# Alternating the two head groups in the chunk scan of a gated-DeltaNet layer

## The chip, the cores and the metric

The program runs on one NeuronCore of a Trainium2 chip, as a single launch. The metric is the device time of that launch in microseconds (us), lower is better. The engines are called as in the profile: PE is TensorE (its weight loads are shown apart as PEld), DVE is VectorE, ACT is ScalarE, POOL is GpSimd, and SP issues DMAs.

## The reference

A trunk of two layers over 512 tokens with 1024 features. Layer 0 is a gated-DeltaNet layer (6 heads of width 128), layer 1 is sliding-window attention; each is followed by a feed-forward part. The change concerns the DeltaNet layer alone. Its state update runs over chunks of tokens, one after the other for each head, and the heads do not depend on each other:

```python
def gated_delta_rule_chunked(q, k, v, g, beta):
    ...
    sol = lax.linalg.triangular_solve(lower, rhs, left_side=True, lower=True, unit_diagonal=True)
    u, w = sol[..., :dv], sol[..., dv:]
    ...
    def step(state, inp):
        u_n, w_n, a_n, qg_n, kg_n, gl_n = inp
        v_new = u_n - jnp.einsum("bhck,bhkv->bhcv", w_n, state)
        o_n = jnp.einsum("bhck,bhkv->bhcv", qg_n, state) + jnp.einsum("bhcs,bhsv->bhcv", a_n, v_new)
        state = state * gl_n[..., None, None] + jnp.einsum("bhck,bhcv->bhkv", kg_n, v_new)
        return state, o_n
```

Afterwards each head's output is normalised, multiplied by a gate `silu(z)`, and projected by `w_out` together with the memory attention.

## The kernel before, in words

Everything is held transposed: features on the 128 partitions, the 512 tokens along the free axis. A dense projection of one 128-wide output tile is 24 matmuls of 128x512: 8 pieces of the inner dimension, times three products, because weights and activations are split into a rounded high part (`whi`, `h`) and the rest (`wlo`, `l`). The function `mm3` issues the three; their results are the PSUM banks called `pj` or `g`. Each weight tile is loaded by SP (`wraw`), rounded by ACT (`whi`) and subtracted by DVE (`wlo`).

The kernel uses chunks of 128 tokens, so there are NC = 4 chunks for each of the 6 heads. The names in the rows of a trace are these: `kn` holds a head's keys, `kg` the decayed keys, `qg` the decayed queries (in the buffers `gcr`, where the output is written over them), `DT` the decayed query-key products, `Tt` the inverted triangles, `N` the values, `S` the state. One step of the scan, for one head and one chunk (`scan_step`, lines 771 to 797), is a chain of small matmuls and small operations of the other engines, all in one PSUM bank `sc`:

- PE `sc<-S,kn`, then DVE `R` (line 781); the first chunk has no state and starts at the next matmul with `N` in place of `R` (`sc<-N,Tt`);
- PE `sc<-R,Tt`, then ACT `vn` (a copy with a factor, line 784);
- PE `sc<-vn,kg`, then DVE `S`, the next state (lines 790, 792); the last chunk has none;
- PE `sc<-gcr,S` and `sc<-DT,vn` give the output, which ACT copies into `gcr` (line 796). Only then is the bank free.

There are three `sc` banks (`self.banks(pj=3, g=2, sc=3)`), and a step keeps one from its first matmul to its copy. A 128x128 matmul on f32 data is two records in the trace; a step has 3 (first chunk), 5, 5 and 4 (last chunk) matmuls, 17 for each head and 102 for the six.

The heads are handled in two groups, `first` (heads 0 to 2) and `second` (heads 3 to 5). `values(heads)` projects a group's values: for each head a projection `pj`, a convolution on ACT and DVE (`qv`), a Silu on ACT, four transposes on PE into a `g` bank and a multiplication on DVE into `N`. After the scan, `squares`, `total` and `finish` normalise a group's output: ACT squares it into `N`, DVE adds and multiplies with tiles that SP has loaded into the buffers of `kg` (`q2`) and `kn` (`z`), PE sums over the partitions with a matmul by `ones` (128x512 on f32 data), ACT takes Ln and Exp, DVE multiplies, and ACT and DVE split the result into `h` and `l`. `opened_rows` then multiplies the parts of the result that are ready by `w_out`, row by row.

The order of the instructions on each engine is not the order of the code. A scheduler of the language orders them when the program is built, by the code's order and by what each waits for; on the chip each engine takes its list strictly in that order. This is how matmuls of a projection come to stand between the steps of a scan. `self.use(LN_EXP)` (line 689) places a load of ACT's function table behind the last Silu and ahead of the first Ln.

Of the kernel before, what the change touches and what calls it, by code (L numbers as in the profile page):

```python
# [23 lines left out]
NC = 4  # L24
# [63 lines left out]
class Builder:  # L88
# [409 lines left out]
    def gdn(self, gp):  # L498
# [112 lines left out]
        for i in range(NH):  # L611
            h, c = divmod(i, NC)
# [14 lines left out]
        def values(heads):  # L627
            vs = {}

            def value(h):  # L630
                vs[h] = self.conv_tile(2 * H + h, self.t(gp, [P, T], F32, "qv", 5))
                self.fn(vs[h], vs[h], AF.Silu)

            value(heads[0])
            for h in heads:
                if h + 1 in heads:
                    value(h + 1)
                v = vs[h]
                ps = self.bank("g")
                for c in range(NC):  # L640
                    self.tr(ps[:, chunk(c)], v[:, chunk(c)])
                self.tt(nc.vector, N[h], c4(ps), wide(ir[h]), ALU.mult)
                vt.append(N[h])
# [4 lines left out]
        def scan(heads, chunks=range(NC)):  # L648
            for c in chunks:
                for h in heads:  # L650
                    S[h] = self.scan_step(gp, h, c, S[h], kn[h], Tt[h], kg[h], vt[h], qg[h], AT[h], br[h])
# [4 lines left out]
        def squares(heads):  # L656
            for h in heads:
                t, gate[h] = self.t(gp, [P, T], F32, f"kg{h}"), self.t(gp, [P, T], F32, f"kn{h}")
                nc.sync.dma_start(t, q2[h])
                nc.sync.dma_start(gate[h], z[h])  # L660
                sums[h], o = (x.rearrange("p c i -> p (c i)") for x in (N[h], qg[h]))
                self.square(sums[h], o)
                self.tt(nc.vector, sums[h], sums[h], t, ALU.add)
            for h in heads:
                o = qg[h].rearrange("p c i -> p (c i)")
                self.tt(nc.vector, o, o, gate[h], ALU.mult)
# [15 lines left out]
        first, second = range(0, 3), range(3, H)  # L682
        for heads in (first, second):
            self.solve(gp, heads, [N[h] for h in heads], X, [Tt[h] for h in heads])
        values(first)
        scan(first, range(NC - 1))
        values(second)
        scan(first, range(NC - 1, NC))
        self.use(LN_EXP)
        scan(second)  # L690
        squares(first)
        total(first, "g")
        finish(first)
# [688 lines left out]
```

## Time and profile before

| | |
|---|---|
| median of 3 runs | 1141.31 us (1141.19 to 1141.54) |
| the profiled execution | 1140.89 us |
| its span, from the first to the last instruction | 1139.0 us |
| PE busy | 1121.6 us, 98% of the span |
| DVE, ACT, POOL busy | 841.6, 632.1, 86.2 us |
| granted clock of TensorE, mean | 0.998 |

The profile's lists by time give the start of an instruction, its length, its engine, its line, what it writes and reads, and in brackets how long the engine stood idle before it and for whom. PE's lengths are modelled and overlap, so that its busy share stays near 100% where it waits for a tenth of a microsecond; its pace is read from one start to the next.

### The profile page before, as it was taken

The numbers are of one execution on the slowest core, as the hardware profiler recorded it, in microseconds if no ns is written. First come the engines' busy times: TensorE is split into PE (matmuls) and PEld (weight loads), VectorE is DVE, ScalarE is ACT, GpSimd is POOL, SyncE is SP. The second block draws the span as 40 slices with busy tenths as digits, with TensorE's granted clock in tenths as the row PEclk, the third lists the DMA queues.
The fourth block names the chain that finished last, engine by engine and source line by source line (L and its number), as shares of the span: only waits on it lengthen the run. The fifth ranks groups of instructions, "written<-read, shape, count | busy, mean of one in ns | idle before, by whom it ended". The sixth has DMA issues, their size and how long they took to land.

```text
span 1139.0 us, 19670 instructions
## 1 busy us (share of the span) xinstructions
PE 1121.6 (98%) x7476; PEld 992.7 (87%) x7476; DVE 841.6 (74%) x1592; ACT 632.1 (55%) x1274; POOL 86.2 (8%) x97
## 2 busy tenths in 40 slices
PE   7999999999999999999999999999999999999996
PEld 6888887887899998899998888888999988999986
DVE  6754887776889987389876868959799743899754
ACT  7569572365566653256653656855566522566533
POOL 0120000000101100011100000010011100111000
PEclk9999999999999999999999999999999999999999
DMA  8434342324667744567723421153477733677232
GB/s 311 128 114 113 120 107 98 95 91 148 188 145 188 186 129 126 159 146 188 185 72 93 134 74 57 43 133 122 126 183 179 199 98 106 150 185 185 70 99 91
DMA packets 73971, 152.76 MB, mean 134 GB/s; under 512 B 17756, under 2 KB 18420, under 8 KB 73876
## 3 DMA queue, kind: packets, MB, share of 16 engines
q1 hardware_dynamic: 62356, 130.52, 37.4%
q0 software_dynamic: 11520, 20.98, 11.7%
q8 instruction: 59, 0.97, 0.4%
q14 instruction: 36, 0.29, 0.1%
HBM read 144.51 MB, written 6.96 MB: 133 GB/s over the span
## 4 chain that ended last, share of the span: by engine, by line
PE 95%; DVE 2%; ACT 1%; DMA 1%; issue 0%; SPq 0%; DVEq 0%; ACTq 0%
PE pj L154 47%; PE g L154 37%; PE sc L154 6%; PE pt L154 2%; PE qk L154 2%; PE pt L168 1%; PE g L168 1%; DMA wraw<-in_wmk 1%; DVE wlo L171 1%; ACT whi L148 0%; ACT sm L142 0%; SPq L329 0%; DVE x L171 0%; DVE l L174 0%; DVE stats L836 0%
## 5 line engine op out<-in xcount | busy, mean ns | idle before, releaser
L148 ACT ACTIVATE whi<-wraw 128x512 fp32r<-128x512 f32 (+2 forms) x331 | 244.1, 746 | 241.9 <-PE pj L154 151.2
L171 DVE TENSOR_TENSOR wlo<-wraw,whi 128x512 fp32r<-128x512 f32 (+2 forms) x331 | 273.0, 835 | 105.8 <-ACT whi L148 99.8
L154 PE MATMUL pj<-h,whi 128*128 128x512 f32 (+1 forms) x676 | 265.4, 393 | 0.1
L154 PE MATMUL pj<-l,whi 128*128 128x512 f32 (+1 forms) x676 | 263.7, 390 | 0.0
L154 PE MATMUL pj<-h,wlo 128*128 128x512 f32 (+1 forms) x676 | 263.4, 390 | 0.0
L154 PE MATMUL g<-T,whi 128*128 128x256 f32 x1280 | 228.1, 278 | 0.2
L154 PEld LDWEIGHTS g<-T,whi 128*128 128x128 f32 x1280 | 194.7, 188 | 1.8 <-DVE fu L174 1.8
L154 PE MATMUL g<-T,wlo 128*128 128x256 f32 x640 | 177.8, 278 | 0.0
L154 PEld LDWEIGHTS pj<-h,whi 128*128 128x128 f32 x676 | 126.9, 188 | 28.4 <-issue 3.5
L154 PEld LDWEIGHTS pj<-h,wlo 128*128 128x128 f32 x676 | 127.0, 188 | 25.8 <-DVE wlo L171 0.4
L154 PEld LDWEIGHTS pj<-l,whi 128*128 128x128 f32 x676 | 127.1, 188 | 24.7 <-DVE l L171 0.4
L154 PE MATMUL g<-h,whi 128*128 128x256 f32 (+1 forms) x492 | 138.4, 281 | 0.0
L154 PE MATMUL g<-h,wlo 128*128 128x256 f32 (+1 forms) x492 | 138.0, 280 | 0.0
L154 PE MATMUL g<-l,whi 128*128 128x256 f32 (+1 forms) x492 | 138.0, 280 | 0.0
L154 PEld LDWEIGHTS g<-T,wlo 128*128 128x128 f32 x640 | 120.1, 188 | 0.0
L154 PEld LDWEIGHTS g<-l,whi 128*128 128x128 f32 x492 | 92.3, 188 | 0.8 <-issue 0.2
L154 PEld LDWEIGHTS g<-h,whi 128*128 128x128 f32 x492 | 92.3, 188 | 0.8 <-issue 0.2
L154 PEld LDWEIGHTS g<-h,wlo 128*128 128x128 f32 x492 | 92.3, 188 | 0.5
L1104 POOL DMA_DIRECT2D ws<-in_wgu x40 | 35.3, 882 | 705.7 <-ACT sq L151 237.7
L148 ACT ACTIVATE whi<-ws 128x512 fp32r<-128x512 f32 x80 | 50.4, 631 | 49.3 <-PE g L154 40.2
L171 DVE TENSOR_TENSOR fu<-pj,rstd 128x512 f32<-128x512 f32 (+1 forms) x34 | 22.4, 660 | 54.3 <-PE pj L154 54.2
L171 DVE TENSOR_TENSOR wlo<-ws,whi 128x512 fp32r<-128x512 f32 x80 | 54.9, 686 | 6.4 <-ACT whi L148 6.3
(384 smaller groups left out, 1649.4 us busy)
## 6 DMA issues: line engine op xcount, KB each, us to landing
wraw<-in_wgu SPq DMA_DIRECT2D x48, 512.0 KB, 4.3
ws<-in_wgu SPq DMA_DIRECT2D x80, 256.0 KB, 3.6
ws<-in_wgu POOLq DMA_DIRECT2D x80, 256.0 KB, 4.9
wraw<-in_wdn SPq DMA_DIRECT2D x48, 384.0 KB, 3.2
wraw<-in_win SPq DMA_DIRECT2D x26, 512.0 KB, 3.6
wraw<-in_wgu SPq DMA_DIRECT2D x40, 256.0 KB, 4.7
wraw<-in_wout SPq DMA_DIRECT2D x16, 512.0 KB, 3.6
wraw<-in_wdn SPq DMA_DIRECT2D x16, 256.0 KB, 2.7
```

Of the source, the lines that this page charges most:

```text
L148: self.copied = self.nc.scalar.activation(out, in_, AF.Copy, **kw).ins
L154: return self.chained(self.nc.tensor.matmul(out, lhsT, rhs, start=start, stop=stop, skip_group_check=more).ins)
L168: return self.chained(self.nc.tensor.transpose(out, in_, self.ident[:k, :k]).ins)
L171: return eng.tensor_tensor(out=out, in0=a, in1=b, op=op).ins
L1104: nc.gpsimd.dma_start(s1, a22, accum_op=ALU.add)
```

## The change

The code that orders the scans at the end of `gdn` is rewritten:

```diff
         values(first)
-        scan(first, range(NC - 1))
+        scan(first, range(2))
         values(second)
-        scan(first, range(NC - 1, NC))
+        for c in (2, 3):
+            scan(first, [c])
+            scan(second, [c - 2])
         self.use(LN_EXP)
-        scan(second)
+        scan(second, range(2, NC))
         squares(first)
```

Before, the first group's chunks 0 to 2 come ahead of the second group's values, its chunk 3 behind them, and then all four chunks of the second group. Now only chunks 0 and 1 of the first group come ahead of the values; then chunk 2 of the first group, chunk 0 of the second, chunk 3 of the first, chunk 1 of the second, and chunks 2 and 3 of the second. No instruction is added or taken away: each engine has as many rows as before, and POOL's are the same in the same order.

Three places show what the lists of the engines make of it. The number behind a name tells buffers apart. The first place is PE during the projection of head 4's values (the second projection of the second group; `h`, `l` times `whi`, `wlo`). In the order before, the steps of chunk 1 and chunk 2 of the first group stand inside it:

```order
L154 MATMUL pj_2387<-h_471,whi_2383 128x512
L154 MATMUL sc_2291<-gcr_101_532,S_2261 128x128
L154 MATMUL sc_2291<-DT_107_538,vn_2296 128x128
L154 MATMUL sc_2304<-gcr_99_530,S_2273 128x128
L154 MATMUL sc_2304<-DT_105_536,vn_2309 128x128
L154 MATMUL sc_2317<-gcr_100_531,S_2286 128x128
L154 MATMUL sc_2317<-DT_106_537,vn_2322 128x128
L154 MATMUL sc_2330<-S_2299,kn_135_660 128x128
L154 MATMUL pj_2387<-l_472,whi_2383 128x512
```

In the order now, the same stretch of that projection holds the end of chunk 1 of head 2 alone:

```order
L154 MATMUL pj_2348<-h_471,whi_2344 128x512
L154 MATMUL sc_2291<-vn_2296,kg_152_754 128x128
L154 MATMUL pj_2348<-l_472,whi_2344 128x512
L154 MATMUL pj_2348<-h_471,wlo_2345 128x512
L154 MATMUL pj_2348<-h_476,whi_2344 128x512
L154 MATMUL sc_2291<-gcr_101_532,S_2261 128x128
L154 MATMUL sc_2291<-DT_107_538,vn_2296 128x128
L154 MATMUL pj_2348<-l_477,whi_2344 128x512
```

Fifteen small matmuls (chunk 2 of the three heads) have moved out of the projections to behind them. The second place is PE behind the transposes of head 5's values (`g_2466` before, `g_2427` now). Before, the first steps of the second group alternate with 128x512 matmuls:

```order
L168 MATMUL g_2466<-consts_66,qv_2423 128x128 x4
L154 MATMUL sc_2512<-N_543,Tt_1422 128x128
L154 MATMUL pj_2714<-mq0h_1203,wlo_2711 128x512
L154 MATMUL pj_2714<-mq1h_1238,whi_2710 128x512
L154 MATMUL g_2659<-N_543,ones_70 128x512
L154 MATMUL sc_2503<-vn_2505,kg_163_806 128x128
L154 MATMUL sc_2512<-vn_2514,kg_174_858 128x128
L154 MATMUL sc_2521<-N_543,Tt_1422 128x128
L154 MATMUL pj_2714<-mq1l_1239,whi_2710 128x512
```

Now two of these matmuls are left there, and behind them come 29 small ones in a row, of all six heads:

```order
L168 MATMUL g_2427<-consts_66,qv_2384 128x128 x4
L154 MATMUL sc_2446<-gcr_100_531,S_2286 128x128
L154 MATMUL sc_2446<-DT_106_537,vn_2451 128x128
L154 MATMUL pj_2714<-mq1l_1239,whi_2710 128x512
L154 MATMUL pj_2714<-mq1h_1238,wlo_2711 128x512
L154 MATMUL sc_2481<-N_543,Tt_1422 128x128
L154 MATMUL sc_2459<-vn_2464,kg_152_754 128x128
L154 MATMUL sc_2472<-vn_2474,kg_163_806 128x128
L154 MATMUL sc_2481<-vn_2483,kg_174_858 128x128
L154 MATMUL sc_2459<-gcr_101_532,S_2299 128x128
L154 MATMUL sc_2459<-DT_107_538,vn_2464 128x128
```

The 128x512 matmuls of `w_out` that stood between them have moved to the end of the scan, ahead of the sums by `ones` of the second group. The third place is ACT around its table load. Before:

```order
L142 ACTIVATE qv_2423<-qv_2423 128x512
L148 ACTIVATE gcr_100_531<-sc_2482 128x128
L133 ACT_TABLE_LOAD
L148 ACTIVATE gcr_101_532<-sc_2492 128x128
L148 ACTIVATE vn_2505<-sc_2503,f_886 128x128
L148 ACTIVATE vn_2514<-sc_2512,f_886 128x128
L151 ACTIVATE N_543<-gcr_100_531 128x512
```

and now:

```order
L142 ACTIVATE qv_2384<-qv_2384 128x512
L133 ACT_TABLE_LOAD
L148 ACTIVATE gcr_100_531<-sc_2446 128x128
L148 ACTIVATE vn_2464<-sc_2459,f_886 128x128
L148 ACTIVATE vn_2474<-sc_2472,f_886 128x128
L148 ACTIVATE vn_2483<-sc_2481,f_886 128x128
L148 ACTIVATE gcr_101_532<-sc_2459 128x128
```

The copy of head 1's output (`gcr_100`), which frees its bank, now stands behind the table load, and three `vn` follow it.

## The prediction

> **What bounds the kernel now.** I read the page first, then the busy time by stretches, then the list by time around the scan. On the page, the busy shares and the chain of work that ended last:
>
> ```profile
> PE 1121.6 (98%) x7476; PEld 992.7 (87%) x7476; DVE 841.6 (74%) x1592; ACT 632.1 (55%) x1274; POOL 86.2 (8%) x97
> PE 95%; DVE 2%; ACT 1%; DMA 1%; issue 0%; SPq 0%; DVEq 0%; ACTq 0%
> ```
>
> PE is the bound, and the change takes no instruction from it. So the question is how long PE waits in the stretch that is reordered. Three stretches, with the busy time of PE, PEld, DVE, ACT and POOL:
>
> ```profile
> 223.08:239.01 15.93, 15.93 (x91) 13.47 (x90) 8.64 (x17) 5.66 (x14) 0.00 (x0) 1.00 0.38 116
> 239.01:266.57 27.56, 27.56 (x177) 23.19 (x176) 21.50 (x45) 19.83 (x49) 0.00 (x0) 1.00 0.33 106
> 266.57:277.46 10.89, 10.89 (x43) 7.74 (x42) 5.51 (x9) 6.68 (x11) 0.00 (x0) 1.00 0.31 93
> ```
>
> The first begins where the two orders part on PE and ends at the transposes of head 4's values; the second ends at the second group's first sum by `ones`, from where the orders are the same again. The third is only there to show what follows. PE counts as busy throughout, so its waits have to be found from its pace. Rows where nothing waits, start and length:
>
> ```profile
> 222.42 0.39 PE L154 MATMUL sc<-gcr,S 128*128 128x128 f32 x2
> 222.64 0.39 PE L154 MATMUL sc<-DT,vn 128*128 128x128 f32 x2
> 222.86 1.02 PE L154 MATMUL sc<-S,kn 128*128 128x128 f32 x6
> 238.10 0.39 PE L154 MATMUL pj<-h,wlo 128*128 128x512 f32 x1
> 238.33 0.39 PE L154 MATMUL pj<-h,whi 128*128 128x512 f32 x1
> 238.55 0.39 PE L154 MATMUL pj<-l,whi 128*128 128x512 f32 x1
> 239.01 0.60 PE L168 MATMUL g<-consts,qv 128*128 128x128 f32 x4
> 239.45 0.83 PE L154 MATMUL sc<-S,kn 128*128 128x128 f32 x6
> 266.57 2.74 PE L154 MATMUL sc<-N,ones 128*128 128x512 f32 x6
> 269.38 0.39 PE L154 MATMUL g<-l,whi 128*128 128x512 f32 x1
> ```
>
> From start to start, a scan matmul (two records) takes 0.224 us, a 128x512 matmul 0.227, four transposes 0.44, and three sums by `ones` 2.58 (2.81 less the one matmul of 0.227 between the two last rows), 0.86 each. The two reordered stretches hold 171 PE rows of the order: 82 scan matmuls (18.37 us), 83 of 128x512 (18.84), 3 times four transposes (1.32) and 3 sums (2.58), together 41.1 us. They took 43.49. So 2.4 us, 0.2% of the whole, is all that waits and uneven pace cost there, and all that any reordering can win.
>
> **The change part by part.** *What moves out of the projections.* In the first stretch 19 scan matmuls become 4: chunk 2 of the first group, 15 matmuls of 0.224 = 3.36 us, moves behind the transposes. Before, this stretch has 15.3 us of work (19 scan matmuls, 47 of 128x512, one set of transposes) and took 15.93: 0.6 lost. With 4 scan matmuls, each with three 128x512 ones between, PE has 0.69 us of other work while a result is fetched. What a step needs is shown by one that ran alone among such matmuls:
>
> ```profile
> 228.62 0.39 PE L154 MATMUL sc<-S,kn 128*128 128x128 f32 x2
> 229.04 0.35 DVE L174 SCALAR_TENSOR_TENSOR R<-sc,negc,N 128x128 f32<-128x128 f32 x1 [1.92 <-PE sc L154]
> 229.54 0.40 PE L154 MATMUL sc<-R,Tt 128*128 128x128 f32 x2
> 230.04 0.37 ACT L148 ACTIVATE vn<-sc,f 128x128 f32<-128x128 f32 x1 [0.94 <-PE sc L154]
> 230.48 0.47 PE L154 MATMUL sc<-vn,kg 128*128 128x128 f32 x2
> 230.98 0.35 DVE L174 SCALAR_TENSOR_TENSOR S<-S,egl,sc 128x128 f32<-128x128 f32 x1 [1.59 <-PE sc L154]
> 231.71 0.39 PE L154 MATMUL sc<-DT,vn 128*128 128x128 f32 x2
> 232.13 0.28 ACT L148 ACTIVATE gcr<-sc 128x128 f32<-128x128 f32 x1 [1.73 <-PE sc L154]
> ```
>
> A consumer starts 0.42 to 0.50 us after its matmul, R and S take 0.35, `vn` 0.37, the copy 0.28. Three matmuls cover nearly all of it, so I keep 0.13 of the 0.6 lost (4/19 of it) and gain 0.47.
>
> *What the second stretch gets.* Its 63 scan matmuls become 78, and the 128x512 matmuls stay 36 in number, but 16 of them (3.63 us) now stand together at its end, where 10 stood before: behind the last step nothing is to be hidden, and the sums by `ones` have 3.6 us of cover in place of 2.3. Inside, 20 are left, and 29 scan matmuls follow one another with none between. There a step has only the other heads' steps as cover, and what a wait costs is seen here:
>
> ```profile
> 254.35 0.28 ACT L148 ACTIVATE gcr<-sc 128x128 f32<-128x128 f32 x1 [0.17 <-PE sc L154]
> 254.38 0.80 PE L154 MATMUL sc<-S,kn 128*128 128x128 f32 x4
> 254.93 0.47 PE L154 MATMUL pj<-l,whi 128*128 128x512 f32 x1
> 256.12 0.28 ACT L148 ACTIVATE gcr<-sc 128x128 f32<-128x128 f32 x1 [0.97 <-PE sc L154]
> 256.45 0.49 PE L154 MATMUL sc<-S,kn 128*128 128x128 f32 x2
> 257.01 0.61 PE L154 MATMUL sc<-vn,kg 128*128 128x128 f32 x4
> 257.38 0.48 PE L154 MATMUL pj<-l,whi 128*128 128x512 f32 x1
> ```
>
> Two scan matmuls and the next start take 0.37 us (257.01 to 257.38); where the second waits for a bank they take 0.55 (254.38 to 254.93). The copy that frees the bank ends at 254.63 and 256.40, and PE starts 0.05 behind it. So a wait costs until 0.05 behind its releaser, and some 0.1 more because the second record comes late too.
>
> With these lengths I went through the new lists of PE, ACT and DVE by hand, from the transposes of head 4's values on, set to 239.01. Each engine takes its list in order, and successive operations overlap by 0.1 us. Twelve PE rows come out late. The costliest is head 4's first matmul, whose bank waits for head 1's copy behind the table load:
>
> ```profile
> 243.75 0.62 ACT L142 ACTIVATE qv<-qv 128x512 f32<-128x512 f32 x1
> 244.55 1.28 ACT L133 ACT_TABLE_LOAD   x1
> 245.85 0.28 ACT L148 ACTIVATE gcr<-sc 128x128 f32<-128x128 f32 x1
> ```
>
> The Silu of head 5's values ends at the same 244.37 in the walk; the load ends at 245.83, the copy at 246.13, and PE, done with its two fillers at 245.83, starts at 246.18: 0.35 + 0.10 = 0.45. Next: the first matmul of head 4's chunk 1 waits for a copy behind a 0.62 square, 0.43; the output matmul of head 2's chunk 3 behind the next square, 0.27; `sc<-vn,kg` of head 4 and head 5, 0.27 and 0.25; the first matmul of heads 3 and 5, 0.17 and 0.18, and of head 5's chunk 1, 0.16; three late bank or `vn` waits in chunks 2 and 3, 0.52 together; the transposes 0.04. Sum 2.74. The second stretch has 78 x 0.224 + 36 x 0.227 + 0.88 + 2.58 = 29.1 us of work; with 2.74 of waits and 0.15 of uneven pace (a few ns at each row) it takes 32.0, where before 25.7 of work took 27.56. The 0.15 is my choice: the lost time before is 0.03 us for each scan matmul in both stretches (0.6/19, 1.8/63), but most of that is waits of the same kind.
>
> *Sum.* First stretch -3.36 - 0.47, second +32.0 - 27.56 = +4.44: **+0.6 us**. To this 0.2 for waits that my walk, which starts every operation as early as it can, leaves out: +0.8. Bounds: if the lost time goes by the number of scan matmuls, 82 before and after, the change is 0; if the walk's waits all come on top of that pace (82 x 0.03 + 2.74 = 5.2 lost, against 2.4), it is +2.8; if all waits vanished, -2.4. I am nearer to the walk's end since it names each wait.
>
> *What else moves, at no cost.* The Silus, the table load and the square/Ln/Exp of the first group stay in their places on ACT up to small shifts. SP issues two `w_out` tiles ahead of the loads for `squares`, and these become free later with their steps. Their landing times:
>
> ```profile
> kg<-q SPq DMA_DIRECT2D x6, 256.0 KB, 3.0
> kn<-z SPq DMA_DIRECT2D x6, 256.0 KB, 3.4
> ```
>
> The latest, head 5's gate, is freed at 264.8 in the walk, lands at 268.2 and is used at 269.5; 1.3 us hide it. POOL's list is unchanged. Behind the sums the chain Ln, Exp, `h` and its cover of 2.0 us are as before.
>
> **A rule of the Trainium skill against a row.** The switch of tables cost 1.48 us here (244.37 to 245.85). The Trainium skill, page "ScalarE: Activation LUTs", section "What ACT_TABLE_LOAD costs", gives some 1.28 us for the load and as much again for a drain, 2.66 in all. The 1.28 agrees; the drain does not show. By the Trainium skill's figure the copy would come 1.2 us later and the time would be 1143.3 us, an estimate; I keep the row.
>
> **The rivals.** *Slower: the banks bind.* Three `sc` banks carry 18 steps from the transposes on, where 15 stood. Before, they go from the `sc<-S,kn` at 239.45 to the end of this copy:
>
> ```profile
> 264.46 0.28 ACT L148 ACTIVATE gcr<-sc 128x128 f32<-128x128 f32 x1 [0.28 <-PE sc L154]
> ```
>
> 25.3 us, so a step holds a bank for 3 x 25.3/15 = 5.06 us. My walk needs 28.3 us for 18, or 4.72 each. If a step still holds its bank for 5.06, the steps end 2.0 us later and nothing behind them gives it back: +2.8, **1144.1 us**. It decides from 4.97 us on. For it: the copies that free the banks stand behind the 0.62 us squares, Ln and Exp on ACT. Against: a step then has fewer 128x512 matmuls inside (20 for 18 steps, before 26 for 15).
>
> *Faster: the two groups mesh.* Six independent chains give PE always something ready, and half of the 2.4 us goes: -1.2, **1140.1 us**. For it: DVE is idle 6 of the 27.6 us. Against: the lists are fixed, and one late row holds all behind it.
>
> *The change does nothing.* The order mixes projections and steps anyway, and the lost time stays 0.03 per scan matmul: **1141.3 us**.
>
> *Slower: the clock drops* in the part with many small waits; 5 us of work at half the granted clock would cost 2.5 us more, **1144.6 us** with the +0.8. Against: the rows of the stretches give a granted clock of 1.00, with waits of this kind in them. The Trainium skill, page "TensorE: Matmul & The Clock Gate", section "A second HAM failure mode: psum-queue depth-cycling", tells of PE idling briefly and often around PSUM and being slowed by its gate; the granted clock above speaks against it here.
>
> **How the numbers follow.** The profiled execution took 1140.89 us, the median of the runs is 0.4 above. 1141.31 + 0.8 = **1142.1 us**. A measurement of this kernel can tell some 0.2%, or 2.28 us, from no change. Chances: my forecast (-0.6 to +2.0) 0.64, all within the bound; the banks 0.17, of which 0.15 slower; the meshing 0.12, of which 0.03 faster; nothing 0.05; the clock 0.02, slower. So faster 0.03, same 0.80, slower 0.17. The range leaves out the greater part of the clock's case and the ends of the bank's and the meshing's: **1140.0 to 1144.4**; the forecast's own is 1140.7 to 1143.3.
>
> **What would show it.** In the profile after: the projections of heads 4 and 5 at 0.227 us a matmul without gaps and the transposes of head 4 some 3.8 us earlier (about 235.2); head 4's first `sc<-N,Tt` right behind the copy that follows the table load; the second stretch near 32.0 us; the sums by `ones` with PE at full pace ahead of them; rows from there on as before. Wrong would be: a second stretch beyond 33.5 us (the banks), one below 30.5 (the meshing), a granted clock below 1.00 in it, or a difference that arises outside the two stretches.

## The result and the profile after

The changed kernel takes 1142.46 us (median of 21 runs, 1141.99 to 1143.4), the kernel before 1141.18 us (21 runs, 1140.65 to 1141.85): a ratio of 1.0013, 95% interval 1.0007 to 1.0019. That is 1.3 us by the medians: a small slowdown that the interval sets clear of no change, and less than the 0.2% that the prediction had set as its bound. The forecast was 1142.1 us and "same". Its sign, place and kind of mechanism hold; its size was too small, +0.8 us for a measured +1.3 by the medians.

The profiled execution of after took 1142.44 us, with a span of 1140.7 (before 1139.0). Its busy shares and the chain of work that ended last, as on the page:

```profile
PE 1122.3 (98%) x7476; PEld 992.4 (87%) x7476; DVE 841.8 (74%) x1592; ACT 633.1 (56%) x1274; POOL 86.1 (8%) x97
PE 95%; DVE 2%; ACT 1%; DMA 1%; issue 0%; SPq 0%; DVEq 0%; ACTq 0%
```

The same work, the same bound. The busy time by stretches shows where the time went. The three rows answer to those of before: from the point where the orders part to head 4's transposes, from there to the second group's first sum by `ones`, and what follows.

```profile
223.18:235.45 12.27, 12.27 (x62) 9.91 (x60) 6.90 (x11) 3.85 (x8) 0.00 (x0) 1.00 0.28 87
235.45:268.09 32.64, 32.07 (x207) 26.89 (x206) 23.61 (x51) 22.17 (x55) 0.00 (x0) 1.00 0.38 113
268.09:278.98 10.89, 10.89 (x43) 7.77 (x42) 5.07 (x8) 6.64 (x11) 0.00 (x0) 1.00 0.29 83
```

The first stretch is 3.66 us shorter (15.93 to 12.27), the second 5.08 longer (27.56 to 32.64): +1.42 together, of the 1.7 by which the spans differ; 0.1 arises ahead of them and 0.2 behind the third row. The third is 10.89 in both. The granted clock is 1.00 throughout. PE is busy 32.07 of 32.64 us, so 0.57 us is idle time that even the page's modelled lengths show, where before had none.

The list by time of PE and ACT in the second stretch, around the table load and the first two squares:

```profile
240.16 0.62 ACT L142 ACTIVATE qv<-qv 128x512 f32<-128x512 f32 x1
240.80 1.28 ACT L133 ACT_TABLE_LOAD   x1
242.00 0.40 PE L154 MATMUL pj<-mq1h,wlo 128*128 128x512 f32 x1
242.09 0.28 ACT L148 ACTIVATE gcr<-sc 128x128 f32<-128x128 f32 x1
242.42 0.49 PE L154 MATMUL sc<-N,Tt 128*128 128x128 f32 x2
242.75 1.11 PE L154 MATMUL sc<-vn,kg 128*128 128x128 f32 x6
243.69 0.41 PE L154 MATMUL sc<-gcr,S 128*128 128x128 f32 x2
...
246.44 0.63 ACT L148 ACTIVATE vn<-sc,f 128x128 f32<-128x128 f32 x2 [0.86 <-PE sc L154]
246.50 0.49 PE L154 MATMUL sc<-DT,vn 128*128 128x128 f32 x2
246.86 0.49 PE L154 MATMUL sc<-gcr,S 128*128 128x128 f32 x2
247.19 0.39 PE L154 MATMUL sc<-DT,vn 128*128 128x128 f32 x2
...
247.86 0.61 PE L154 MATMUL sc<-S,kn 128*128 128x128 f32 x4
247.92 0.63 ACT L151 ACTIVATE N<-gcr 128x512 f32<-128x512 f32 x1
248.46 0.26 ACT L148 ACTIVATE gcr<-sc 128x128 f32<-128x128 f32 x1
248.77 0.49 PE L154 MATMUL sc<-S,kn 128*128 128x128 f32 x2 [0.30 <-ACT gcr L148]
249.09 0.61 PE L154 MATMUL sc<-R,Tt 128*128 128x128 f32 x4
249.52 0.63 ACT L148 ACTIVATE vn<-sc,f 128x128 f32<-128x128 f32 x2
249.94 0.49 PE L154 MATMUL sc<-gcr,S 128*128 128x128 f32 x2 [0.23 <-ACT vn L148]
250.26 0.39 PE L154 MATMUL sc<-DT,vn 128*128 128x128 f32 x2
```

Read it from start to start, at 0.224 us for each scan matmul (a row with x6 is three of them). The filler at 242.00 is done at 242.23, and head 4's first matmul starts at 242.42, behind the copy of head 1 that had to wait for the table load: 0.19, and 0.10 more because its second record comes late (0.33 to the next start). The two costliest waits are lower down. At 247.86 two matmuls take 0.91: the third would have started at 248.31, but the copy that frees its bank stands behind a square on ACT and ends at 248.72, so PE starts at 248.77: 0.46 + 0.10. At 249.09 two matmuls take 0.85, because `vn` is ready only at 249.89: 0.40 + 0.10.

### The profile page after: what moved, and what is told of

Read it like the earlier page. It is cut to its first block, busy times and chain, and to the rows that moved or that the text cites. A ratio compares the mean times of both kernels' runs of the same rounds, so it can differ in the third digit from the quotient of the medians.

```text
span 1140.7 us, 19668 instructions
## 1 busy us (share of the span) xinstructions
PE 1122.3 (98%) x7476; PEld 992.4 (87%) x7476; DVE 841.8 (74%) x1592; ACT 633.1 (56%) x1274; POOL 86.1 (8%) x97
## 4 chain that ended last, share of the span: by engine, by line
PE 95%; DVE 2%; ACT 1%; DMA 1%; issue 0%; SPq 0%; DVEq 0%; ACTq 0%
PE pj L154 47%; PE g L154 37%; PE sc L154 6%; PE pt L154 2%; PE qk L154 2%; PE pt L168 1%; PE g L168 1%; DMA wraw<-in_wmk 1%; DVE wlo L171 1%; ACT whi L148 0%; ACT sm L142 0%; SPq L329 0%; DVE x L171 0%; DVE l L174 0%; DVE stats L838 0%
```

## The experiments

All comparisons of times are with the kernel before, run on the same chip. Since the differences are near what the times can tell, each profile is also read at one place, called the scan's stretch: from the transposes of head 2's values to the second group's first sum by `ones`. For before and for after:

```profile
217.37:266.57 49.20, 49.20 (x306) 41.76 (x306) 33.30 (x68) 28.59 (x70) 0.00 (x0) 1.00 0.31 98
```

```profile
217.46:268.09 50.63, 50.06 (x306) 41.91 (x306) 33.67 (x68) 29.13 (x70) 0.00 (x0) 1.00 0.31 95
```

The change costs 1.43 us by this measure. It is one profiled execution each, so differences of 0.1 us mean little.

**Without the alternation.** Chunk 2 of the first group still moves behind the values, but the groups don't alternate. Against the changed kernel:

```diff
-        for c in (2, 3):
-            scan(first, [c])
-            scan(second, [c - 2])
+        scan(first, (2, 3))
         self.use(LN_EXP)
-        scan(second, range(2, NC))
+        scan(second)
```

> Chunks 2 and 3 of the first group both behind the second group's values, as in the changed kernel, but all ahead of the second group's chunks: no alternation. The longest run of scan matmuls without a 128x512 one on PE falls from 29 to 13. Theory (the time is lost in the long run, where only other heads' steps cover a wait): the second stretch loses about 0.8 us less, 1141.6 us (ratio 1.0005). Rival A (it is lost because chunk 2 has left the projections, alternation or not): like the changed kernel, 1142.5 us (1.0013). Rival B (three banks bind, since 18 steps go through them behind the projections): 1142.5 us too.

1141.9 us against 1140.81, ratio 1.0009 (1.0001 to 1.0018), between what the two views asked. The longest run of scan matmuls came out at 14. The scan's stretch:

```profile
217.44:267.80 50.36, 49.74 (x306) 41.81 (x306) 33.60 (x68) 29.03 (x70) 0.00 (x0) 1.00 0.30 95
```

50.36 us, 0.27 less than after and 1.16 more than before. So most of the cost is there without any alternation, and comes already when chunk 2 leaves the projections. My theory had put it on the long run of 29. Inside the new run of 14 and behind it PE again waits for banks:

```profile
245.09 0.63 ACT L151 ACTIVATE N<-gcr 128x512 f32<-128x512 f32 x1
245.26 0.39 PE L154 MATMUL sc<-N,Tt 128*128 128x128 f32 x2
245.63 0.26 ACT L148 ACTIVATE gcr<-sc 128x128 f32<-128x128 f32 x1
245.94 0.49 PE L154 MATMUL sc<-N,Tt 128*128 128x128 f32 x2 [0.30 <-ACT gcr L148]
```

The matmul at 245.26 is done at 245.48. The next one needs the bank that the copy frees, the copy stands behind a square, and PE starts at 245.94: 0.46 us late. A wait of 0.48 us for a copy behind an Ln follows at 249.94.

**The table load later.** Against the changed kernel, the load is placed behind the copies of the second group's chunk 0:

```diff
             scan(second, [c - 2])
+            if c == 2:
+                held = self.copied
         self.use(LN_EXP)
+        self.nosync(self.table_ins, held)
```

> The changed kernel with ACT's table load held back until the second group's chunk 0 has been copied out. Theory: head 1's copy comes some 1.4 us sooner, head 4's first matmul no longer waits for it, 0.3 to 0.45 us less, 1142.0 us (ratio 1.0008), unless the load now stands ahead of another copy, and then the same wait shows there. Rival A and B: no change, 1142.5 us (1.0013).

1141.77 us against 1140.81, ratio 1.0008 (0.9999 to 1.0017); the stretch is 50.24, or 0.39 less, as expected. The list by time shows how:

```profile
241.82 0.28 ACT L148 ACTIVATE gcr<-sc 128x128 f32<-128x128 f32 x1 [0.28 <-PE sc L154]
242.15 0.49 PE L154 MATMUL sc<-N,Tt 128*128 128x128 f32 x2
...
246.55 1.28 ACT L133 ACT_TABLE_LOAD   x1
...
246.86 0.39 PE L154 MATMUL sc<-S,kn 128*128 128x128 f32 x2
247.29 0.35 DVE L174 SCALAR_TENSOR_TENSOR R<-sc,negc,N 128x128 f32<-128x128 f32 x1 [1.10 <-PE sc L154]
247.69 0.49 PE L154 MATMUL sc<-R,Tt 128*128 128x128 f32 x2 [0.45 <-DVE R L174]
247.84 0.28 ACT L148 ACTIVATE gcr<-sc 128x128 f32<-128x128 f32 x1
248.17 0.49 PE L154 MATMUL sc<-S,kn 128*128 128x128 f32 x2
```

Head 4's first matmul now starts right behind its copy, and nearly without a wait. But the list is ordered differently further down, and two waits arise there. The matmul at 246.86 is done at 247.08, and the next one needs the `R` that DVE makes of its result: it starts at 247.69, and 0.6 us are lost with nothing between the two. This wait is not the load's, it only falls into the same time. The copy at 247.84 does stand behind the load, and PE's matmul at 248.17, which waits for it, comes 0.26 late. What the move saves, it saves net of these.

**The squares off ACT.** The squares that stand ahead of the late copies go to POOL:

```diff
-                self.square(sums[h], o)
+                self.tt(nc.gpsimd, sums[h], o, o, ALU.mult)
```

> The changed kernel with the squares of both groups as multiplications on POOL in place of ACT. Theory: the copies that free the banks in the first group's chunk 3 stand behind no square of 0.63 us on ACT; the two longest waits of PE (at 248.8 and 249.9 us, some 0.5 each) shrink to 0.1 or 0.2 us: 0.6 us less, 1141.9 us (ratio 1.0006), less whatever the longer operation on POOL (1.3 to 1.5 us) costs at the second group's end, where it has 3.6 us of cover. Rival A and B: no change, 1142.5 us (1.0013).

1141.81 us against 1140.81, ratio 1.0009 (1.0 to 1.0019); the stretch is 50.36, or 0.27 less, where 0.6 was expected. The same place:

```profile
247.72 1.02 PE L154 MATMUL sc<-S,kn 128*128 128x128 f32 x6
247.93 0.28 ACT L148 ACTIVATE gcr<-sc 128x128 f32<-128x128 f32 x1 [0.17 <-PE sc L154]
248.58 1.09 PE L154 MATMUL sc<-R,Tt 128*128 128x128 f32 x6
249.56 0.49 PE L154 MATMUL sc<-gcr,S 128*128 128x128 f32 x2
249.88 0.39 PE L154 MATMUL sc<-DT,vn 128*128 128x128 f32 x2
```

The two big waits are gone: three `sc<-S,kn` take 0.86 (work 0.67) and three `sc<-R,Tt` 0.98. Each of these rows is still 0.2 to 0.3 late, and the matmul at 249.56 again takes 0.32: once ACT is quicker, the chain from matmul to `R` and from matmul to `vn` is the next to be late. The 30 scan matmuls in a row here (6.72 us of work) take 8.68 us, where the 29 of after (6.50 us of work) take 8.92. So the place gains 0.46 us of the 0.6 expected, and 0.2 is lost again elsewhere in the stretch.

**The heads spread.** An order that should beat both, made from the one before:

```diff
-        values(second)
+        values(range(3, 5))
         scan(first, range(NC - 1, NC))
+        scan(range(3, 5), [0])
+        values(range(5, H))
+        scan(range(5, H), [0])
         self.use(LN_EXP)
-        scan(second)
+        scan(second, range(1, NC))
```

> From the kernel before: heads 3 and 4 are projected first, then come the first group's chunk 3 and chunk 0 of heads 3 and 4, and only then head 5's values; so the steps fall among the 24 matmuls of head 5's projection, and the longest run of scan matmuls without a 128x512 one or a sum is 10. Theory: fewer waits than before, 0.5 to 1 us less, 1140.5 us (ratio 0.9994). Rival A: like before, 1141.2 (1.0000), since chunk 2 lies in the projections as before. Rival B: as many steps behind the projections as before less 5: somewhat faster, 1140.7 us.

1144.66 us against 1140.81, ratio 1.003 (1.0019 to 1.0042): a miss with the wrong sign. The list by time ahead of head 5's transposes:

```profile
243.75 1.06 ACT L148 ACTIVATE whi<-wraw 128x1024 fp32r<-128x1024 f32 x1 [0.42 <-PE pj L154]
...
244.71 0.67 ACT L148 ACTIVATE qv<-pj,gains 128x512 f32<-128x512 f32 x1
244.84 1.23 DVE L171 TENSOR_TENSOR wlo<-wraw,whi 128x1024 fp32r<-128x1024 f32 x1 [1.65 <-ACT whi L148]
...
245.98 2.31 DVE L174 SCALAR_TENSOR_TENSOR qv<-pj,gains,qv 128x511 f32<-128x511 f32 x3
...
248.39 0.63 ACT L142 ACTIVATE qv<-qv 128x512 f32<-128x512 f32 x1 [3.00 <-DVE qv L174]
249.04 1.28 ACT L133 ACT_TABLE_LOAD   x1
249.07 0.66 PE L168 MATMUL g<-consts,qv 128*128 128x128 f32 x4 [2.40 <-ACT qv L142]
```

Behind head 5's projection come a copy, three taps on DVE (2.31) and a Silu. The copy waits until ACT has rounded a weight tile, and the taps until DVE has subtracted one, so that it takes 5.1 us, from 243.94 to 249.07. PE has only twelve 128x512 matmuls (2.7 us) to put there, the last at 246.28. In the kernels before and after, the scan of chunk 3 or of other heads stands there. The steps of a scan don't only need cover; they are cover for the convolution. The profiled execution took 1143.1 us; the further 1.5 us of the median stay unexplained, since no trace shows them.

**Four banks, before and after.** To separate the wait for banks from the wait for results, one bank moves from the projections to the scan, in the kernel before and in the changed one:

```diff
-                with self.banks(pj=3, g=2, sc=3):
+                with self.banks(pj=2, g=2, sc=4):
```

In the kernel before:

> The kernel before with four sc banks and two pj banks in place of three and three: the control of the next run. Both theories: within 0.5 us of before, 1140.8 us (ratio 1.0000); two pj banks may cost some tenths where a projection waits for its bank.

In the changed kernel:

> The changed kernel with four sc banks and two pj banks. Rival B (the number of banks binds the alternated scan): the change then costs nothing, within 0.3 us of the control. Theory (a run of scan matmuls with no 128x512 one between is what costs, through whatever is late on ACT and DVE; banks are one such wait of several): the longest run is now 15, so that about half of the 1.4 us stays, 0.5 to 0.8 us over the control.

The times as wholes, 1149.18 and 1153.76 us (ratios 1.0067, 1.0041 to 1.0094, and 1.0094, 1.0066 to 1.0122), say nothing of the scan: two `pj` banks cost PE 2.7 and 3.8 us of idle time between 100 and 200 us, where before has none, and in the first of the two the granted clock fell well ahead of the scan (told at the end). The scan's stretch ran at a clock of 1.00 in both. Before with four banks, then after with four:

```profile
230.49:278.61 48.12, 48.12 (x305) 40.96 (x305) 32.77 (x68) 28.54 (x69) 0.00 (x0) 1.00 0.31 99
```

```profile
223.50:272.57 49.07, 48.66 (x305) 41.35 (x305) 33.08 (x68) 27.88 (x69) 0.00 (x0) 1.00 0.30 97
```

With a fourth bank the stretch is faster in both (0.23 us of it is one 128x512 matmul that now lies ahead of it), and the change still costs 0.95 us between them, where three banks give 1.43. The rival in which banks are everything asked for 0.3 at most, and falls; my own 0.5 to 0.8 was too low. How much of the cost is the banks' this doesn't settle: the lists are ordered anew with four banks, and in the changed kernel the longest run of scan matmuls is then 15 in place of 29. A share of a third, by 0.95 against 1.43, is an estimate that includes the new order.

**Two orders between.** In the first, the order of before with head 3's chunk 0 ahead of the projection of head 5; in the second, also chunk 2 of the first group a projection later in the code than before, but still ahead of the projections of heads 4 and 5. The second, against before:

```diff
-        scan(first, range(NC - 1))
-        values(second)
+        scan(first, range(2))
+        values([3])
+        scan(first, [2])
+        values([4])
+        scan([3], [0])
+        values(range(5, H))
         scan(first, range(NC - 1, NC))
         self.use(LN_EXP)
-        scan(second)
+        scan(range(4, H), [0])
+        scan(second, range(1, NC))
```

> From the kernel before: heads 3 and 4 projected, chunk 0 of head 3 during head 5's projection, then the first group's chunk 3 with 15 matmuls of 128x512 over the time that head 5's values need on DVE and ACT, then the rest. So the transposes of head 5 have 6.8 us of PE work ahead of them (in the run with heads 3 and 4 early it was 3.0, and PE stood for 2.6). Theory: the longest run of scan matmuls is 8, the lost time of the two stretches falls from 2.4 to about 1.8 us, 1140.3 us (ratio 0.9995). Rival A and B: as before, 1140.8 us (1.0000).

> As the last one, with chunk 2 of the first group behind head 3's values instead of ahead of them, in the projections of heads 4 and 5. Theory: as the last one, 1140.3 us (0.9995), since cover is the same. Rival A (chunk 2 later is what costs): 0.5 us more than the last one.

1141.24 and 1141.15 us against 1141.14, both with a ratio of 1.0000 (0.9991 to 1.0009 and 0.9991 to 1.0008): no gain, so a miss for the first. The stretch of the second:

```profile
217.40:266.84 49.44, 49.44 (x307) 41.22 (x307) 32.94 (x68) 28.72 (x70) 0.00 (x0) 1.00 0.31 97
```

49.44 us (the first has 49.42), 0.24 above before. But this run is no test of a later chunk 2, since on PE's list it has hardly moved. Of the 55 projection matmuls that follow head 2's transposes, 20, 20 and 24 stand ahead of the outputs of its three heads, and 17, 17 and 26 in before. So whether chunk 2 may come later at no cost, as long as it stays ahead of the last projection, isn't shown. What the two runs do say is that the order of before gains nothing from an earlier chunk 0 of head 3. No order tried beats the one before.

**Six extra matmuls.** If PE waits in the changed order, then work added there must be partly free. Against each of the two kernels, in `scan_step`:

```diff
         self.mm(ps[:, 1, :], Tt[:, c, :], R)
+        if c == 0 and h >= 3:
+            self.mm(ps[:, 0, :], Tt[:, c, :], R)
...
+        if c == NC - 1 and h < 3:
+            self.mm(ps[:, 3, :], AT[:, c, :], v)
         if S is not None:
             self.mm(ps[:, 2, :], S, qg[:, c, :], True, False)
```

> The changed kernel with six more scan-size matmuls whose results nobody reads: one behind each first matmul of the second group's chunk 0 (same operands), one ahead of the last two of each step of the first group's chunk 3. Work added to PE: 6 x 0.224 = 1.34 us. My theory: in the run without 128x512 matmuls PE waits for the other engines (3.4 us of waits by the trace), so part of the added work falls into idle time: the scan's stretch grows by 0.5 to 0.9 us over the changed kernel's 50.63, to 51.1 to 51.5. Rival, PE is full and the loss is only slower pace of its rows: it grows by 1.3 or more, to 52.0.

> The kernel before with the same six matmuls. Both theories: here the steps have 128x512 matmuls around them and PE waits little, so the stretch grows by 1.1 to 1.4 us over 49.20, to 50.3 to 50.6. If it grows as little as in the changed kernel, the wait time isn't what sets the two orders apart.

The stretch of after with the six, then of before with them:

```profile
217.85:268.92 51.07, 50.96 (x318) 43.18 (x318) 34.33 (x68) 29.18 (x70) 0.00 (x0) 1.00 0.31 94
```

```profile
217.74:268.17 50.43, 50.41 (x318) 43.05 (x318) 33.66 (x68) 28.64 (x70) 0.00 (x0) 1.00 0.30 95
```

1.34 us of work lengthens the changed kernel's stretch by 0.44 (50.63 to 51.07, a little under the 0.5 to 0.9 expected), and that of before by 1.23. So 0.9 us of it cost nothing in the changed order, and 0.1 in the order before; the two orders now differ by 0.64 us in place of 1.43. The times are 1143.12 and 1142.34 us against 1140.89, ratios 1.0019 (1.001 to 1.0028) and 1.0012 (1.0003 to 1.0021). By these medians the six matmuls cost 0.95 and 1.45 us, so 0.5 us was free in the changed order: the same direction and a smaller size, within what the intervals allow.

The rival of a full PE at a slower pace asked for 1.3 or more, and falls. Not all of the 0.9 need be idle time that was filled, since the lists are ordered anew: between the first and the last step behind head 4's transposes there are 24 matmuls of 128x512 in place of 20 in the changed kernel, and 23 in place of 26 in before. Together with the late rows of the list above, the test says that the cost of the change is for the larger part idle time of PE.

## Why the prediction held, and where its size was off

*That a reorder can only move PE's waits, 2.4 us of which there were.* Held: equal work, a clock of 1.00, and the same time behind the sums within 0.2 us. Two reordered stretches of 43.49 us became 44.91.

*First stretch, -3.36 - 0.47.* 12.27 us came for a forecast of 12.1, a gain of 3.66 for 3.83. Its work is 12.0 us, so 0.26 stayed lost and not 0.13. Head 4's transposes stand at 235.45, forecast "about 235.2", of which 0.10 lies ahead of the stretch.

*Second stretch, 32.0.* It came at 32.64, inside the bounds of 30.5 and 33.5 that I had set for it. The work is 29.1, so waits and uneven pace took 3.5 and not 2.9. **The term that came out too small is the sum of 2.74 over the twelve late rows**, and the rows shown above tell which terms were off. Each term below is the lateness of a row and of the one after it.

- `sc<-gcr,S` of head 2's chunk 3 (at 249.94): forecast 0.27, came 0.50. I had put the wait for `vn` on the matmul that reads `vn`, and so counted `sc<-gcr,S` ahead of it as 0.22 of cover (the prediction's text says only "the output matmul"). The profile has the wait at `sc<-gcr,S`, one matmul sooner.
- The same at 246.86, in the first group's chunk 3, behind the `vn` that starts at 246.44: 0.24. The prediction names no such wait, unless it is one of the "three late bank or `vn` waits" that it gives as 0.52 together. The row ahead of it, at 246.50, comes late too, by some 0.1.
- The first matmul of head 4's chunk 1 (at 248.77) behind the square: forecast 0.43, came 0.56.
- Head 4's first matmul behind the table load: forecast 0.45, came 0.29. PE came to it when the walk had it, and the copy 0.2 sooner: the switch cost 1.31 us here (the Silu ends at 240.78, the copy starts at 242.09). The 1.48 that I had read off the kernel before was too long, since a copy of 0.27 stands there between the Silu and the load (third place of the change above).
- The three `sc<-vn,kg` behind it: 0.94 us from 242.75 to 243.69 for 0.67 of work, so 0.27, forecast 0.27.

The first three add 0.6 us at most, the fourth takes 0.16, so that errors of both signs stand in the sum. The other late rows that the prediction names one by one are within 0.1 of it.

*The 0.2 for waits that the walk leaves out.* Too small: the walk's +0.6 became +1.42, so 0.8 was wanted. A walk that starts each operation as early as it can is a lower bound where its prices are right, and the larger part of what it missed here came from one wait read at the wrong instruction, which occurs twice.

*The banks, forecast as a rival with 0.17.* They didn't bind on the whole: from the start of the scan at 235.88 to the last copy's end at 265.28 there are 18 steps in three banks, so a step holds its bank for 3 x 29.4/18 = 4.90 us, under the 4.97 from which that rival was to decide, and over the walk's 4.72. But single steps do wait for a bank: the 0.56 at 248.77 and the 0.29 at 242.42 are such waits, and with four banks the cost falls from 1.43 to 0.95. So my line between "the walk" and "the banks" was too sharp: both waits are at work in the same rows.

*The meshing, nothing, the clock.* The first two fall by +1.42 us at a place where the meshing asked for -1.2 and the other for 0. The clock falls by 1.00 in both stretches, in spite of a dozen waits of 0.1 to 0.5 us within 10 us: the rule of the Trainium skill that I weighed there (page "TensorE: Matmul & The Clock Gate", section "A second HAM failure mode: psum-queue depth-cycling") did not show itself here. The price that I had put on this rival was too low: at a clock of 0.50 a 128x512 matmul takes 0.43 us in place of 0.227 (last section), so 5 us of work would cost some 5 us more, and not 2.5.

*The table load.* The Trainium skill, page "ScalarE: Activation LUTs", section "What ACT_TABLE_LOAD costs", has a drain beside the load. In after the load takes 1.28 us and the copy starts 1.29 behind the load's start: the load agrees, and a drain does not show.

*What I had not argued and the runs showed.* I explained the second stretch by the run of 29 scan matmuls. PE does lose most there: from 242.42 to 251.34 it takes 8.92 us for 6.50 us of work, 2.4 of the 3.5 us lost. But without the alternation the longest run is 14, with 25 matmuls of 128x512 among the steps (20 in after, 26 in before), and 1.16 of the 1.43 us remain. Both orders have 78 scan matmuls behind the last projection, where before has 63. That this number sets the cost is argued from these orders; the runs don't part it from the banks and from copies that come late on ACT.

## What to carry to other kernels

In a chain of small dependent steps on an engine that is the bound, count the independent work left beside them: moving 15 small matmuls from a place with cover to one without cost more than the place had gained, even though the groups that then alternate are independent of each other. When you walk a list by hand, look up in the trace on which instruction each wait sits, since it can be one ahead of the reader of the data, and expect the walk's sum to be too low. To tell waiting from pace, add a known amount of work at the place: what is free was idle time, as far as the list's order stays the same, so compare the lists.

## What the runs showed of the hardware

- An engine's copies are quick, and still late: the 0.26 us copy at 248.46 cost PE 0.56 us, since it stood behind a 0.63 square, and a wait of PE delays the second record of the matmul too (0.32 to 0.33 us to the next start in place of 0.224).
- The granted clock fell to half for some 20 us in the kernel before with four banks, a stretch in which DMA moved nothing for 15 us and PE counts as busy. From 197.7 to 217.6 a 128x512 matmul takes 0.43 us from start to start in place of 0.227. The rows by windows (us, PE, PEld, DVE, ACT, POOL, clock, DMA share, GB/s):

```profile
148.00:150.00 2.00, 2.00 (x22) 1.65 (x24) 2.00 (x4) 0.99 (x2) 0.00 (x0) 0.87 0.19 62
150.00:160.00 10.00, 10.00 (x45) 7.74 (x42) 5.23 (x15) 7.78 (x23) 0.00 (x0) 0.85 0.73 129
...
200.00:205.00 5.00, 5.00 (x67) 3.70 (x67) 2.65 (x10) 0.00 (x0) 0.00 (x0) 0.50 0.00 0
...
210.00:215.00 5.00, 5.00 (x29) 4.31 (x28) 3.88 (x7) 0.00 (x0) 0.00 (x0) 0.50 0.00 0
```

  PE had stood idle for 2.58 us just ahead of 147.96, and the clock is lower from 148 on (0.87 and 0.85); the drop at 197.7 has no such wait ahead of it. A wait of 2.40 us in the kernel with the heads spread was followed by a clock of 1.00. So a long wait of PE may or may not be followed by a lower clock here; what decides it stays open.
